# A compact triangular inverse on 32- and 64-row tiles, masks on VectorE, and part of the weights' low parts on GpSimd

## Chip, cores and metric

One NeuronCore of a Trainium2 chip runs the whole program as one launch. The metric is the device time in microseconds (us), the median of three runs. Engines by name: TensorE (PE, and PEld for its weight loads), VectorE (DVE), ScalarE (ACT), GpSimd (POOL), and SyncE (SP), which issues the transfers of the weights.

## What is computed

Two transformer blocks over 256 tokens of width 2048, in fp32. Block 1 mixes a gated linear recurrence, forgetting attention and a pooling branch, then a feed-forward of 5632. Block 2, which the change touches, mixes 16 heads of an RWKV-7 recurrence (head size 64) with 8 heads of a gated delta rule (GDN, head size 128), then projects out and runs a second feed-forward. Cut to what matters:

```python
h = rms_norm_2(x, attn_norm_w); proj = h @ w_in            # 2048 -> 3360 + 3088
y_a = rwkv7_mixer(proj[..., :N_RWKV_IN], ...)              # S = S*w + (S a) b^T + v k^T, y = S r
y_b = gdn_mixer(proj[..., N_RWKV_IN:N_IN], ...)            # chunked delta rule:
#   L = tril(k_beta k^T * gamma, -1); u, w = solve(I + L, [v_beta, k_beta * exp(g)])
x = x + concat([y_a, y_b]) @ w_out
x = x + (silu(h2 @ w_gate) * (h2 @ w_up)) @ w_down         # h2 = rms_norm_2(x, ffn_norm_w)
```

Both mixers are computed in chunks of 128 tokens. Each chunk of each head then needs the inverse of a 128x128 unit triangular matrix; the kernel calls the strictly triangular matrices `ab`, and four of them (two heads, two chunks) make one inverse step.

## The kernel before, in words

**Products.** Weights are streamed once, as tiles of 128 output columns by up to eight k-tiles of 128 (chunks of 128x1024 fp32). `weights` (L302) starts a chunk's transfer on SyncE, rounds it on ScalarE to a high part `hi` in fp32r (L314), and subtracts on VectorE to get the low part `lo` (L315, listed under L206). `product` multiplies: per k-tile, `step3` issues a 512-column matmul of hi against the activations' two parts and a 256-column matmul of lo against their high part. The rings hold 4 raw, 3 hi and 3 lo chunks. ScalarE and VectorE work on chunks ahead of TensorE by a priority offset (`ahead_mix`, 139 and 145 in the mixers).

**Order of the work.** In block 2 the program is written in sequence, and a list scheduler orders each engine's instructions at build time by priority and by its own estimate of times; `high_priority(offset=n)` moves what stands in it ahead of the code around it. At run time every engine works its list in order and waits on semaphores.

**The mixers** (`mixers`, L898) have four groups, each of two RWKV head pairs and then two GDN heads. For each: the projections (`rwkv_front`, `gdn_front`: the products, the token shift or convolution, the decay, the matrices `ab`), then `diagonals`, later `merged_inverse` and the back part (`rwkv_back`, `gdn_back`). The back part of one half group is issued beside the projections of the next, with `back_ahead` = 205; `diagonals` stands 129 ahead. There are 12 inverse steps: 8 for RWKV, 4 for GDN. The last GDN back part stands after `out2_first`, the first 12 k-tiles of the output projection (L1399); `out2_second` does the last 4.

**The inverse.** `diagonals` (L1098) sends the 16x16 diagonal blocks through DRAM, inverts them on VectorE, and brings them back as `cm`. `merged_inverse` (L1127) spreads these over a 128x128 block-diagonal `xt` with a mask on VectorE, transposes it to `x` on TensorE (L236) and copies that on ScalarE (L1139). Two levels follow, 16 and 32: VectorE masks `ab` to `off`, TensorE multiplies `off` by `x`, then the result `m1` by `xt` (four full 128x128 products each), and transposes the new `xt` (L1163; full tiles at level 16, 64x64 at level 32). For RWKV, VectorE adds the identity to `m1` and ScalarE copies `xt`; for GDN, ScalarE scales `m1` by beta and VectorE adds to `xt`. The last level joins the two 64-row halves with 64x64 products.

**GpSimd** does only small memsets in the mixers (L962, L1011, L1280), and adds squares in `out2_second`.

The lines that the core of the steps rests on:

```python
for lev in ("lev16", "lev32"):
    off = self.tp.tile([P, 4, P], F32, name="off", tag="w4")
    self.mul(off, full[:, p0:p0 + 4], self.bc(lev, 4))
    for q in range(4):
        self.mm(pm[:, q * P:(q + 1) * P], off[:, q], x[:, q])
```

Of the kernel before, what the change touches and what calls it, by code (L numbers as in the profile page):

```python
# [7 lines left out]
F32 = mybir.dt.float32  # L8
F32R = mybir.dt.float32r
AF = mybir.ActivationFunctionType  # L10
ALU = mybir.AluOpType
# [4 lines left out]
P = 128  # L16
S = 256
# [134 lines left out]
def constants():  # L152
    i = np.arange(P)
    r, c = i[:, None], i[None, :]
    sel1 = np.zeros((P, 8), np.float32)
    sel2 = np.zeros((P, 8), np.float32)
    for h in range(8):
        sel1[h, h] = 1.0
        sel2[32 + h, h] = 1.0
    c1 = ((i >= 32) & (i < 40)).astype(np.float32)[:, None]  # L160
    c2 = (i < 8).astype(np.float32)[:, None]
    up = (c > r).astype(np.float32)
    upi = (c >= r).astype(np.float32)
    same = lambda b: (r // b == c // b)
    lev = lambda b: (same(2 * b) & ~same(b) & (c > r)).astype(np.float32)
    return [
        ("ident", np.eye(P)), ("ones", np.ones((P, P))),
        ("causal", np.where(c <= r, 0.0, -1e30)), ("causalT", np.where(r <= c, 0.0, -1e30)),
        ("head64", same(64).astype(np.float32)),
        ("nsel1", -sel1), ("sel2", sel2), ("c1", c1), ("c2", c2),  # L170
        ("atmask", np.concatenate([up, upi], 1)),
        ("lev16", lev(16)), ("lev32", lev(32)), ("lev64", lev(64)), ("blk16", same(16).astype(np.float32)),
        ("id16", np.broadcast_to(np.eye(16).reshape(1, 256), (P, 256))),
    ]


def ffn_out(w):
# [5 lines left out]
class Prog:  # L183
# [83 lines left out]
    pieces = (4, 4, 4, 4)  # L267
    early = []
    parted = False
    narrow = nar3 = nar4 = False  # L270
    nar1 = nar2 = nar5 = True
    turn = 0
# [29 lines left out]
    def weights(self, src, nkt):  # L302

        parts = []
        ahead = self.ahead_mix if self.parted else (self.ahead[self.narrow],) * 2
        for k in range(0, nkt, 8):
            n = min(8, nkt - k) * P
            with self.tc.high_priority(offset=ahead[0]):
                raw = self.rawp.tile([P, n], F32, name="raw", tag="raw")
                self.nc.sync.dma_start(out=raw, in_=src[:, k * P:k * P + n])  # L310
            with self.tc.high_priority(offset=ahead[1]):
                hi = self.hip.tile([P, n], F32R, name="hi", tag="hi")
                lo = self.lop.tile([P, n], F32R, name="lo", tag="lo")
# [481 lines left out]
class Block2(Block1):  # L795
# [25 lines left out]
    def block2(self):  # L821
        rh = lambda k, h=self.h: h[:, k]
        with ExitStack() as st:
            self.yp = self.pool("y2", 1, st=st)
            self.y = self.moving(self.yp, 8, "y", at=self.AT["y"])
            self.yg = [None] * 8
            with ExitStack() as st2:
                self.mixers(rh, st2)
            xst = ExitStack()
            self.x = self.pool("xres", 1, st=xst, side="right").tile([P, KT, S], F32, name="xres", tag="xres")  # L830
            self.narrow = self.nar5
            self.out2_second()
        self.narrow = False
        with xst:
            self.ffn("wg2", "wd2", 1e-5, self.feed_out, "left")
            self.last_norm()
# [61 lines left out]
    def mixers(self, rh, st):  # L898
# [24 lines left out]
        for g in range(4):  # L923
            slots = self.rwkv_group(g, rh, w2)
# [8 lines left out]
            self.step(pend, first=True)  # L933
        self.narrow = self.nar4
        self.out2_first()
        self.step(pend)

    def step(self, pend, first=False):
# [14 lines left out]
                        self.gdn_back(g, fr, xx)  # L953

    back_ahead = 205
    diag_ahead = 129
    front_ahead = 0

    def shifted(self, ps, o, j):

        t = self.w(S + 1, "shf")
        self.G.memset(t[:, 0:1], 0.0)  # L962
# [42 lines left out]
    def rwkv_rest(self, j, slot, t, slots):  # L1005
        gp, sg = self.gp, self.sg[j]
        r, k, v = t

        ch = lambda z: z.rearrange("p (c t) -> p c t", c=2)
        cw, e1, e2 = (ch(self.w(2 * (P + 1), n)) for n in ("cw", "e1", "e2"))  # L1010
        self.G.memset(cw[:, :, 0:1], 0.0)  # L1011
# [86 lines left out]
    def diagonals(self, slots, gdn):  # L1098
# [25 lines left out]
        self.nc.sync.dma_start(out=cm, in_=scr2.rearrange("p b i j -> (b i) p j"))  # L1124
        slots["cm"] = cm

    def merged_inverse(self, slots, half, gdn):  # L1127

        full, cm, p0 = slots["ab"], slots["cm"], 4 * half
        q4 = lambda z: z.rearrange("p (q t) -> p q t", q=4)  # L1130
        xt = self.gp.tile([P, 4, P], F32, name="xt", tag="xt", bufs=2)
        x = self.gp.tile([P, 4, P], F32, name="xn", tag="xn", bufs=2)
        self.mul(xt.rearrange("p q (b j) -> p q b j", b=8),
                 cm[:, p0:p0 + 4].rearrange("p q (a j) -> p q a j", a=1).to_broadcast([P, 4, 8, 16]),
                 self.c("blk16").rearrange("p (a b j) -> p a b j", a=1, b=8).to_broadcast([P, 4, 8, 16]))
        px = self.psx_tile(True)
        for q in range(4):
            self.tr(px[:, q * P:(q + 1) * P], xt[:, q])
        self.A.copy(x, q4(px))  # L1139
        beta = lambda q, rows=slice(0, P): self.nbt[rows, q % 2, 2 * gdn + q // 2:2 * gdn + q // 2 + 1]  # L1140
        for lev in ("lev16", "lev32"):
            off = self.tp.tile([P, 4, P], F32, name="off", tag="w4")
            self.mul(off, full[:, p0:p0 + 4], self.bc(lev, 4))
            pm = self.psx_tile(True)
            for q in range(4):
                self.mm(pm[:, q * P:(q + 1) * P], off[:, q], x[:, q])
            m1 = self.tp.tile([P, 4, P], F32, name="m1", tag="w4")
            pt = self.psx_tile(True)
            if gdn is None:
                self.add(m1, q4(pm), self.bc("ident", 4))  # L1150
            else:
                for q in range(4):
                    self.act(m1[:, q], pm[:, q * P:(q + 1) * P], AF.Copy, scale=beta(q))
            for q in range(4):
                self.mm(pt[:, q * P:(q + 1) * P], m1[:, q], xt[:, q])
            if gdn is None:
                self.A.copy(xt, q4(pt))
            else:
                self.add(xt, q4(pt), xt)
            px = self.psx_tile(True)  # L1160
            n = P if lev == "lev16" else 64
            for q in range(4):
                self.T.transpose(px[:n, q * n:(q + 1) * n], xt[:n, q, :n], self.c("ident")[:n, :n])  # L1163
            self.A.copy(x[:n, :, :n], q4(px[:n, :4 * n]))

        lo, hi = slice(0, 64), slice(64, P)
        pm = self.psx_tile(True)
        for q in range(4):
            self.mm(pm[hi, q * 64:(q + 1) * 64], full[lo, p0 + q, hi], x[lo, q, lo])
        m1 = self.tp.tile([P, 4, P], F32, name="m1", tag="w4")  # L1170
        if gdn is None:
            self.A.copy(m1[hi, :, :64], q4(pm[hi, :S]))
        else:
            for q in range(4):
                self.act(m1[hi, q, :64], pm[hi, q * 64:(q + 1) * 64], AF.Copy, scale=beta(q, hi))
        for q in range(4):
            self.mm(pm[lo, S + q * 64:S + (q + 1) * 64], m1[hi, q, :64], xt[hi, q, hi])
        self.A.copy(xt[lo, :, hi], q4(pm[lo, S:]))
        return xt

# [89 lines left out]
    def gdn_front(self, i, rh, w2, slots):  # L1270
# [3 lines left out]
        for b in range(6):  # L1274
# [2 lines left out]
                self.scaled(ps, big[:, b])  # L1277
                continue
            t = self.w(S + 3, f"gc{b}")
            self.G.memset(t[:, :3], 0.0)  # L1280
            self.scaled(ps, t[:, 3:])
            ch = (i, 4 + i, 8 + 2 * i, 9 + 2 * i)[b]
            o = big[:, b]
# [152 lines left out]
```

## Time and profile before

| what | value |
|---|---|
| median of 3 runs | 2920.99 us (2920.43 to 2922.79) |
| the profiled execution | 2924.65 us, span 2922.9 us |
| TensorE busy | 2888.2 us (99%), 17676 matmuls |
| VectorE busy | 1990.9 us (68%) |
| ScalarE busy | 1506.3 us (52%) |
| GpSimd busy | 21.5 us (1%) |
| mean granted TensorE clock | 0.998 of full speed |

The span runs from the first to the last instruction of the profiled execution; its own time is 1.75 us longer. Durations in the trace are of that execution. A matmul's duration holds its way through the array, so neighbours overlap, and TensorE's pace is read from the starts of instructions in a row rather than from their durations.

### The profile page before, as it was taken

The numbers are of one execution on the slowest core, as the hardware profiler recorded it, in microseconds if no ns is written. First come the engines' busy times: TensorE is split into PE (matmuls) and PEld (weight loads), VectorE is DVE, ScalarE is ACT, GpSimd is POOL, SyncE is SP. The second block draws the span as 40 slices with busy tenths as digits, with TensorE's granted clock in tenths as the row PEclk, the third lists the DMA queues.
The fourth block names the chain that finished last, engine by engine and source line by source line (L and its number), as shares of the span: only waits on it lengthen the run. The fifth ranks groups of instructions, "written<-read, shape, count | busy, mean of one in ns | idle before, by whom it ended". The sixth has DMA issues, their size and how long they took to land. (4 is left out here: it accounts for less than half of the span.)

```text
span 2922.9 us, 46401 instructions
## 1 busy us (share of the span) xinstructions
PE 2888.2 (99%) x17676; PEld 2540.8 (87%) x17676; DVE 1990.9 (68%) x3393; ACT 1506.3 (52%) x2448; POOL 21.5 (1%) x88
## 2 busy tenths in 40 slices
PE   8999999999999999999999999999999999999998
PEld 8999988888888888888888878887888888888887
DVE  7855766666766665666667878888776665566665
ACT  6644454444554444444556555666564444444454
POOL 0000000000000000000000000000010000000000
PEclk9999999999999999999999999999999999999999
DMA  6544555555655556555565423233465555655554
GB/s 232 183 160 154 173 188 191 190 188 189 231 190 189 189 177 192 201 191 191 180 206 186 148 87 122 92 130 110 145 207 189 190 186 182 201 191 190 184 177 159
DMA packets 178047, 515.78 MB, mean 176 GB/s; under 512 B 32024, under 2 KB 59040, under 8 KB 177568
## 3 DMA queue, kind: packets, MB, share of 16 engines
q1 hardware_dynamic: 177536, 511.80, 51.9%
q8 instruction: 138, 2.26, 0.3%
q10 hardware_dynamic: 288, 1.02, 0.1%
q14 instruction: 85, 0.70, 0.1%
HBM read 505.66 MB, written 7.09 MB: 175 GB/s over the span
## 5 line engine op out<-in xcount | busy, mean ns | idle before, releaser
L233 PE MATMUL ps<-h,hi 128*128 128x512 f32 (+1 forms) x5904 | 1801.0, 366 | 1.2 <-DVE xp L206 0.9
L206 DVE TENSOR_TENSOR lo<-raw,hi 128x1024 fp32r<-128x1024 f32 (+2 forms) x1028 | 1156.6, 1125 | 759.0 <-ACT hi L314 754.9
L314 ACT CAST hi<-raw 128x1024 fp32r<-128x1024 f32 (+2 forms) x1028 | 997.2, 971 | 1193.3 <-issue 663.8
L233 PE MATMUL ps<-h,lo 128*128 128x256 f32 x5152 | 1410.6, 282 | 0.9 <-DVE lo L206 0.6
L233 PEld LDWEIGHTS ps<-h,hi 128*128 128x128 f32 x5904 | 1041.6, 188 | 164.4 <-issue 6.0
L233 PEld LDWEIGHTS ps<-h,lo 128*128 128x128 f32 x5152 | 969.5, 188 | 29.4 <-issue 2.4
L233 PE MATMUL ps<-mid,hi 128*128 128x512 f32 (+1 forms) x1452 | 486.2, 385 | 0.0
L233 PE MATMUL ps<-mid,lo 128*128 128x256 f32 x1408 | 386.1, 281 | 0.0
L233 PEld LDWEIGHTS ps<-mid,hi 128*128 128x128 f32 x1452 | 265.4, 188 | 50.5
L233 PEld LDWEIGHTS ps<-mid,lo 128*128 128x128 f32 x1408 | 265.1, 188 | 5.3
L206 DVE TENSOR_TENSOR t<-ps,s 128x256 f32<-128x256 f32 x323 | 134.8, 417 | 0.0
L381 ACT COPY s<-ps 128x256 f32<-128x256 f32 x323 | 118.3, 367 | 0.0
L233 PE MATMUL ps<-merged,hi 128*128 128x512 f32 x256 | 88.0, 392 | 0.0
L233 PE MATMUL ps<-merged,lo 128*128 128x256 f32 x256 | 69.0, 280 | 0.0
L233 PEld LDWEIGHTS ps<-merged,hi 128*128 128x128 f32 x256 | 47.0, 188 | 9.6 <-DVE merged L206 0.2
L233 PE MATMUL ps<-y,hi 128*128 128x512 f32 (+1 forms) x160 | 49.3, 359 | 1.7 <-ACT hi L314 1.4
L233 PEld LDWEIGHTS ps<-merged,lo 128*128 128x128 f32 x256 | 48.1, 188 | 1.3
L233 PE MATMUL ps<-yg,hi 128*128 128x512 f32 (+1 forms) x160 | 48.6, 354 | 0.0
L233 PE MATMUL ps<-yb,hi 128*128 128x512 f32 x128 | 46.1, 393 | 0.0
L233 PE MATMUL ps<-yc,hi 128*128 128x512 f32 x128 | 46.1, 393 | 0.0
L233 PE MATMUL ps<-ya,hi 128*128 128x512 f32 x128 | 45.9, 391 | 0.0
L206 DVE TENSOR_TENSOR t<-ps,xres 128x256 f32<-128x256 f32 x78 | 33.1, 424 | 12.9 <-PE ps L233 7.0
(383 smaller groups left out, 2307.8 us busy)
## 6 DMA issues: line engine op xcount, KB each, us to landing
raw<-wg SPq DMA_DIRECT2D x352, 512.0 KB, 4.2
raw<-w SPq DMA_DIRECT2D x292, 512.0 KB, 3.6
raw<-wd SPq DMA_DIRECT2D x128, 512.0 KB, 3.5
raw<-wbr SPq DMA_DIRECT2D x48, 512.0 KB, 3.5
raw<-wo SPq DMA_DIRECT2D x48, 512.0 KB, 4.3
raw<-wd SPq DMA_DIRECT2D x128, 192.0 KB, 3.1
raw<-wo SPq DMA_DIRECT2D x32, 256.0 KB, 3.2
xin<-x SPq DMA_DIRECT2D x4, 512.0 KB, 6.4
```

Source lines behind the costliest of these rows:

```text
L206: return (e or self.V).tensor_tensor(out=o, in0=x, in1=y, op=op)
L233: return self.T.matmul(o, lhsT=l, rhs=r, start=start, stop=stop, skip_group_check=True)
L314: self.A.copy(hi, raw)
L381: self.A.copy(s[:rows], ps[:rows, S:])
```

## The change

The two lower levels of the inverse work on compact tiles: level 16 on four 32x32 diagonal blocks of each matrix, level 32 on two 64x64 blocks. Both the inverse so far and its transpose are kept (`x[:, 0]` and `x[:, 1]`), so the transposes on TensorE go; the first one is VectorE's transpose of 32x32 blocks. The identity is added to `m` in both mixers, and a mask on VectorE spreads a level's blocks into the next tile. The masked `ab` (`off32`, `off64`) are made once per group in `diagonals`. While `shared` is set (from the start of the mixers to the end of `out2_second`), the last 256 columns of the low part of a chunk of over four k-tiles are subtracted on GpSimd. The small memsets go to VectorE, and the last back part gets priority 2000.

```diff
 constants():
-        ("lev16", lev(16)), ("lev32", lev(32)), ("lev64", lev(64)), ("blk16", same(16).astype(np.float32)),
+        ("id64", np.tile(np.eye(64), (2, 1))), ("id32", np.tile(np.eye(32), (4, 1))),
+        ("lev16", diag_blocks(lev(16), 32)), ("lev32", diag_blocks(lev(32), 64)),
+        ("blk16", diag_blocks(same(16).astype(np.float32), 32)), ("blk32", diag_blocks(same(32).astype(np.float32), 64)),
...
+def diag_blocks(m, n):
+    return np.concatenate([m[i:i + n, i:i + n] for i in range(0, P, n)], 0)
 setup():
-        self.cst = self.const.tile([P, a["cst"].shape[1]], F32, name="cst")
+        self.cst = self.const.tile([P, a["cst"].shape[1] + 224], F32, name="cst")[:, :a["cst"].shape[1]]
 weights():
-                self.sub(lo, raw, hi.bitcast(F32))
+                m = n - 2 * P if self.shared and n > 4 * P else n
+                self.sub(lo[:, :m], raw[:, :m], hi[:, :m].bitcast(F32))
+                if m < n:
+                    self.sub(lo[:, m:], raw[:, m:], hi[:, m:].bitcast(F32), self.G)
 mixers():
-        self.parted = True
+        self.parted = self.shared = True
...
         self.out2_first()
+        self.back_ahead = self.last_ahead
         self.step(pend)
...
+    last_ahead = 2000
 shifted(), rwkv_rest(), gdn_front():
-        self.G.memset(...)
+        self.V.memset(...)
 diagonals(), at its end:
+        for lev, w in (("lev16", 32), ("lev32", 64)):
+            off = slots[lev] = gp.tile([P, n, w], F32, name=f"off{w}", tag=f"off{w}_{n}")
+            for r in range(0, P, w):
+                r = slice(r, r + w)
+                self.mul(off[r], full[r, :, r], self.c(lev, r).rearrange("p (a t) -> p a t", a=1).to_broadcast([w, n, w]))
 merged_inverse(), in place of the spread, the transposes and the two levels:
+        def tiles(out, left, right, w, rows=P):
+            for q in range(4):
+                for r in range(0, rows, w):
+                    r = slice(r, r + w)
+                    self.mm(out[r, q], left[r, q], right[r, q])
+        def merge(x, lev, w, rows):
+            off = slots[lev][:, p0:p0 + 4]
+            pm = self.psx_tile(True)
+            tiles(q4(pm[:, :4 * w]), off, x[:, 1], w)
+            m = self.tp.tile([P, 4, 64], F32, name="m1", tag="m4", bufs=3)[:, :, :w]
+            if gdn is None:
+                self.add(m, q4(pm[:, :4 * w]), one(self.c(f"id{w}"), w))
+            else:
+                for q in range(4):
+                    self.stt(m[:, q], pm[:, q * w:(q + 1) * w], beta(q), self.c(f"id{w}"), ALU.mult, ALU.add)
+            pt = self.psx_tile(True)
+            pt = pt[:, :8 * w].rearrange("p (a q t) -> p a q t", a=2, q=4)
+            tiles(pt[:, 0], m, x[:, 0], w)
+            tiles(pt[:, 1], x[:, 0], m, w, rows)
+            return pt
+        xt = self.gp.tile([P, 4, P], F32, name="xt", tag="xt", bufs=2)
+        self.V.memset(xt[hi, :, lo], 0.0)
+        x = self.gp.tile([P, 2, 4, 32], F32, name="xa", tag="xa", bufs=2)
+        self.mul(x[:, 0].rearrange("p q (b j) -> p q b j", b=2),
+                 cm[:, p0:p0 + 4].rearrange("p q (a j) -> p q a j", a=1).to_broadcast([P, 4, 2, 16]),
+                 self.c("blk16").rearrange("p (a b j) -> p a b j", a=1, b=2).to_broadcast([P, 4, 2, 16]))
+        self.V.transpose(x[:, 1].rearrange("p q t -> p (q t)"), x[:, 0].rearrange("p q t -> p (q t)"))
+        pt = merge(x, "lev16", 32, P)
+        x = self.gp.tile([P, 2, 4, 64], F32, name="xb", tag="xb", bufs=1)
+        for j in range(2):
+            self.mul(x[:, j].rearrange("p q (b t) -> p q b t", b=2),
+                     pt[:, j].rearrange("p q (b t) -> p q b t", b=1).to_broadcast([P, 4, 2, 32]),
+                     self.c("blk32").rearrange("p (a b t) -> p a b t", a=1, b=2).to_broadcast([P, 4, 2, 32]))
+        pt = merge(x, "lev32", 64, 64)
+        for r in (lo, hi):
+            self.A.copy(xt[r, :, r], pt[r, 0])
+        y = self.tp.tile([P, 4, 64], F32, name="xc", tag="m4", bufs=3)
+        self.V.tensor_copy(y[lo], pt[lo, 1])
```

The join of the two halves that follows is as before, with `y` in place of `x` and a compact `m1`.

## Rows read from the trace of the kernel before

**Rows 1.** The page, part 1 (busy time of each engine).

```profile
PE 2888.2 (99%) x17676; PEld 2540.8 (87%) x17676; DVE 1990.9 (68%) x3393; ACT 1506.3 (52%) x2448; POOL 21.5 (1%) x88
...
PE 26%; DVE 0%; ACT 0%; DMA 0%; issue 0%; ACTq 0%; POOLq 0%; DVEq 0%
```

**Rows 2.** Stretches: us, then PE, PEld, DVE, ACT, POOL, clock, DMA.

```profile
1440.00:1460.00 20.00, 20.00 (x117) 17.63 (x116) 13.34 (x22) 11.09 (x18) 0.00 (x0) 1.00 0.67 212
...
1680.00:1700.00 20.00, 17.16 (x103) 14.45 (x102) 12.89 (x28) 10.97 (x25) 0.45 (x3) 0.91 0.32 105
...
1780.00:1800.00 20.00, 20.00 (x117) 17.60 (x116) 18.05 (x51) 11.34 (x14) 0.00 (x0) 1.00 0.56 191
...
2020.00:2040.00 20.00, 20.00 (x117) 17.58 (x117) 18.56 (x55) 10.76 (x14) 0.00 (x0) 1.00 0.48 156
...
1580.00:2144.00 564.00, 554.16 (x3446) 458.68 (x3445) 440.50 (x1086) 337.57 (x671) 5.25 (x48) 1.00 0.38 123
```

**Rows 3.** Waits of TensorE, 1575 to 2150 us, the longest group.

```profile
PE pb L236 <- DVE xt L206: 3.5, 4, 2.8
```

**Rows 4.** TensorE's weight loads, 1580 to 2144 us: count, busy us, mean ns, idle before.

```profile
L233 PEld LDWEIGHTS pb<-xt,m 128*128 128x128 f32 x192 | 25.1, 190 | 2.5 <-ACT m L230 1.1 <-issue 0.2
...
L236 PEld LDWEIGHTS pb<-cst,xt 128*128 128x128 f32 x48 | 5.9, 147 | 6.0 <-DVE xt L206 5.5
...
L233 PEld LDWEIGHTS pb<-xn,ab 64*64 64x64 f32 x64 | 4.3, 134 | 1.7 <-issue 1.0 <-ACT s L381 0.2 <-ACT xn L1164 0.2
...
L1163 PEld LDWEIGHTS pb<-cst,xt 64*64 64x64 f32 x48 | 3.0, 107 | 3.4 <-ACT xt L1157 1.7 <-DVE xt L206 1.1 <-issue 0.7
```

**Rows 5.** Timeline of one inverse: start us, us from first to last end, instructions.

```profile
1696.62 0.97 PEld L233 LDWEIGHTS pb<-xt,m 128*128 128x128 f32 x8
...
1699.90 0.39 PE L233 MATMUL ps<-h,hi 128*128 128x512 f32 x1
...
1700.22 0.54 PEld L233 LDWEIGHTS pb<-xn,ab 64*64 64x64 f32 x8 [0.24 <-ACT s L381]
...
1701.05 0.40 PE L233 MATMUL ps<-h,hi 128*128 128x512 f32 x1
```

**Rows 6.** Timeline of the RWKV front: column halves, then row halves.

```profile
1633.68 0.66 PE L233 MATMUL pf<-ak,tok 128*64 128x128 f32 x8
...
1629.11 0.69 PE L233 MATMUL pf<-ar,kt 64*128 64x256 f32 x4
...
1629.54 0.59 PE L233 MATMUL pf<-ar,bt 64*128 64x256 f32 x2
```

**Rows 7.** VectorE's operations by form, 1575 to 2150 us.

```profile
L206 DVE TENSOR_TENSOR lo<-raw,hi 128x1024 fp32r<-128x1024 f32 x111 | 135.3, 1220 | 32.7 <-ACT hi L314 32.5
...
L218 DVE SCALAR_TENSOR_TENSOR ak<-pf,cst 128x256 f32<-128x256 f32 x32 | 13.3, 416 | 0.0
...
L206 DVE TENSOR_TENSOR m<-pb,cst 128x512 f32<-128x512 f32 x16 | 10.9, 684 | 3.4 <-PE pb L233 3.2
...
L206 DVE TENSOR_TENSOR off<-ab,cst 128x512 f32<-128x512 f32 x16 | 10.9, 681 | 0.0
...
L206 DVE TENSOR_TENSOR ar<-r,e 128x128 f32<-128x128 f32 x16 | 4.5, 280 | 0.5 <-ACT e L230 0.5
...
L206 DVE TENSOR_TENSOR etmp<-d,e 32x63 f32<-32x63 f32 x8 | 1.7, 207 | 0.0
...
L206 DVE TENSOR_TENSOR sc<-e,e 128x1 f32<-128x1 f32 x8 | 1.2, 148 | 0.0
```

**Rows 8.** By form: GpSimd 1500 to 2200, VectorE 2144 to 2180, VectorE 700 to 860.

```profile
L206 POOL TENSOR_TENSOR acc<-acc,q 128x256 f32<-128x256 f32 x15 | 13.8, 920 | 154.7 <-ACT q L230 154.7
...
L218 DVE SCALAR_TENSOR_TENSOR h<-xres,par,h 128x256 fp32r<-128x256 f32 x16 | 11.3, 714 | 0.2
...
L218 DVE SCALAR_TENSOR_TENSOR h<-xres,par,h 128x256 fp32r<-128x256 f32 x16 | 7.7, 478 | 0.0
```

More of the change, by code (lines that the diff above doesn't have):

```diff
@@ L269 @@
     parted = False
+    shared = False
     narrow = nar3 = nar4 = False
@@ L832, in block2 @@
             self.out2_second()
-        self.narrow = False
+        self.narrow = self.shared = False
         with xst:
@@ L961, in shifted @@
         t = self.w(S + 1, "shf")
-        self.G.memset(t[:, 0:1], 0.0)
+        self.V.memset(t[:, 0:1], 0.0)
         self.scaled(ps, t[:, 1:])
@@ L1010, in rwkv_rest @@
         cw, e1, e2 = (ch(self.w(2 * (P + 1), n)) for n in ("cw", "e1", "e2"))
-        self.G.memset(cw[:, :, 0:1], 0.0)
+        self.V.memset(cw[:, :, 0:1], 0.0)
         for c in range(2):
@@ L1125, in diagonals @@
         slots["cm"] = cm
+        for lev, w in (("lev16", 32), ("lev32", 64)):
[3 more added lines that the diff above has]
+                self.mul(off[r], full[r, :, r], self.c(lev, r).rearrange("p (a t) -> p a t", a=1).to_broadcast([w, n, w]))
     def merged_inverse(self, slots, half, gdn):
         full, cm, p0 = slots["ab"], slots["cm"], 4 * half
+        lo, hi = slice(0, 64), slice(64, P)
@@ L1130, in merged_inverse @@
         q4 = lambda z: z.rearrange("p (q t) -> p q t", q=4)
[L1131 to L1136, printed above, removed]
@@ L1137, in merged_inverse @@
-        for q in range(4):
-            self.tr(px[:, q * P:(q + 1) * P], xt[:, q])
-        self.A.copy(x, q4(px))
-        beta = lambda q, rows=slice(0, P): self.nbt[rows, q % 2, 2 * gdn + q // 2:2 * gdn + q // 2 + 1]
-        for lev in ("lev16", "lev32"):
-            off = self.tp.tile([P, 4, P], F32, name="off", tag="w4")
-            self.mul(off, full[:, p0:p0 + 4], self.bc(lev, 4))
+        one = lambda z, w: z.rearrange("p (a t) -> p a t", a=1).to_broadcast([P, 4, w])
+        beta = lambda q, rows=slice(0, P): self.nbt[rows, q % 2, 2 * gdn + q // 2:2 * gdn + q // 2 + 1]
@@ L1144, in merged_inverse @@
+        def tiles(out, left, right, w, rows=P):
[5 more added lines that the diff above has]
+            off = slots[lev][:, p0:p0 + 4]
             pm = self.psx_tile(True)
-            for q in range(4):
-                self.mm(pm[:, q * P:(q + 1) * P], off[:, q], x[:, q])
-            m1 = self.tp.tile([P, 4, P], F32, name="m1", tag="w4")
@@ L1148, in merged_inverse @@
-            pt = self.psx_tile(True)
+            tiles(q4(pm[:, :4 * w]), off, x[:, 1], w)
+            m = self.tp.tile([P, 4, 64], F32, name="m1", tag="m4", bufs=3)[:, :, :w]
             if gdn is None:
-                self.add(m1, q4(pm), self.bc("ident", 4))
+                self.add(m, q4(pm[:, :4 * w]), one(self.c(f"id{w}"), w))
             else:
                 for q in range(4):
-                    self.act(m1[:, q], pm[:, q * P:(q + 1) * P], AF.Copy, scale=beta(q))
-            for q in range(4):
-                self.mm(pt[:, q * P:(q + 1) * P], m1[:, q], xt[:, q])
@@ L1156, in merged_inverse @@
[L1156 to L1166, printed above, removed]
+                    self.stt(m[:, q], pm[:, q * w:(q + 1) * w], beta(q), self.c(f"id{w}"), ALU.mult, ALU.add)
@@ L1167, in merged_inverse @@
+        pt = merge(x, "lev32", 64, 64)
[3 more added lines that the diff above has]
+        self.V.tensor_copy(y[lo], pt[lo, 1])
         pm = self.psx_tile(True)
         for q in range(4):
-            self.mm(pm[hi, q * 64:(q + 1) * 64], full[lo, p0 + q, hi], x[lo, q, lo])
-        m1 = self.tp.tile([P, 4, P], F32, name="m1", tag="w4")
+            self.mm(pm[hi, q * 64:(q + 1) * 64], full[lo, p0 + q, hi], y[lo, q])
@@ L1171, in merged_inverse @@
+        m1 = self.tp.tile([P, 4, 64], F32, name="m1", tag="m4", bufs=3)
         if gdn is None:
-            self.A.copy(m1[hi, :, :64], q4(pm[hi, :S]))
+            self.A.copy(m1[hi], q4(pm[hi, :S]))
         else:
             for q in range(4):
-                self.act(m1[hi, q, :64], pm[hi, q * 64:(q + 1) * 64], AF.Copy, scale=beta(q, hi))
+                self.act(m1[hi, q], pm[hi, q * 64:(q + 1) * 64], AF.Copy, scale=beta(q, hi))
         for q in range(4):
-            self.mm(pm[lo, S + q * 64:S + (q + 1) * 64], m1[hi, q, :64], xt[hi, q, hi])
+            self.mm(pm[lo, S + q * 64:S + (q + 1) * 64], m1[hi, q], xt[hi, q, hi])
@@ L1279, in gdn_front @@
             t = self.w(S + 3, f"gc{b}")
-            self.G.memset(t[:, :3], 0.0)
+            self.V.memset(t[:, :3], 0.0)
             self.scaled(ps, t[:, 3:])
```

## Prediction

> **What bounds the kernel now.** I read the page's busy shares and its chain first: TensorE is busy 99% of the span and the chain that ended last is TensorE's products [rows 1]. "Busy" here holds matmul latency, so I next read the table of stretches: a plain product stretch has 117 matmuls in 20 us, that is 0.34 us for a pair of one hi (512 columns) and one lo (256) [rows 2]. The mixers, the only place that the change touches, run from about 1580 to 2144 us: TensorE 554 of 564 us, VectorE 440, ScalarE 338, GpSimd 5 [rows 2]. Then the waits: TensorE's longest group there is 3.5 us, for the first block of the inverse [rows 3]; the stretch 1680 to 1700 that holds it also has the only lower granted clock, 0.91 (a mean of the two levels) against 1.00 elsewhere [rows 2]. So the mixers are bound by TensorE's instruction stream, with VectorE near 90% in places (18.05 and 18.56 of 20 us) [rows 2]. A microsecond taken off TensorE's stream is worth about one, while VectorE keeps up.
>
> **TensorE: what goes.** Each self.mm in fp32 is two instructions. An inverse (12 of them: 8 rwkv, 4 gdn) now issues 4 block transposes, and per level 4+4 products and 4 transposes; the last join (16 instructions of 64x64) stays. Price of one, from eight in a row: full tiles (0.97 - 0.19) / 7 = 0.111 us, 64x64 tiles (0.54 - 0.13) / 7 = 0.058 us [rows 4, 5]. A run of small tiles pays more than its instructions: from the hi before it to the second hi after it are 1.15 us (1699.90 to 1701.05), less the pair's 0.34 and 8 x 0.058 = 0.46, leaves 0.35 us per run for emptying and refilling the array [rows 2, 5]. Gone per inverse: 32 x 0.111 + 8 full transposes x 0.11 (taken at the full tiles' price) + one run of 4 small transposes (0.23 + 0.35) = 3.55 + 0.88 + 0.58 = 5.0 us; times 12 is 60 us (counts: 192, 192, 48, 48 and 48 [rows 4], the second 192 and the second 48 in rows of the same kind).
>
> **TensorE: what comes.** Level 16: 16 + 32 products on 32x32 tiles, 96 instructions; level 32: 8 + 8 + 4 on 64x64, 40 instructions; in four runs. 32 columns stand in no row. Serial price by the line through 0.111 and 0.058: about 0.031 us. Do tiles on different rows and columns of the array run side by side? Column halves do: eight 128x64 instructions take 0.66 us where eight full ones of the same length take 0.97 for their loads alone [rows 5, 6]. Row halves do: four in two tiles take 0.69 us, two in one tile 0.59 [rows 6]. The new tiles are diagonal, apart in both, and neighbours in issue order. Bounds: serial, 96 x 0.031 + 40 x 0.058 + 4 x 0.35 = 6.7 us per inverse, 80 us, a net +20; all tiles side by side (four of 32, two of 64; the last 8 instructions have one tile alone), 0.74 + 0.92 + 0.46 + 1.4 = 3.5 us, 42 us, a net -18; only pairs, 4.3 us, 51 us, a net -9. I take -18: it is what both rows of tiles show, carried from two to four.
>
> **VectorE.** Prices: 512 columns 0.68, 256 0.42, 128 0.28, 63 0.21, one column 0.15, a lo of 1024 1.22, so a lo of 768 between them 0.95 us [rows 7]. Masks move to the step of the diagonals: an rwkv group pays 4 x 0.42 + 2 x 0.68 for 4 x 0.68 before, +0.3; a gdn group 4 x 0.28 + 2 x 0.42 for 2 x 0.68, +0.6. Per inverse three operations of 512 go (-2.0). Come: block spread 0.28, the 32x32 transpose (in no row: 0.15 to 0.68, taken as 0.28 like any 128 columns), zeroing a quarter 0.28 to 0.42, merge one 0.28 (gdn: 4 x 0.21, ScalarE before), two spreads 0.84, merge two 0.42 (gdn 4 x 0.21), one copy 0.42: rwkv +0.8, gdn +1.8. Sum 4 x 0.9 + 8 x 0.8 + 4 x 1.8 = +17 us. 48 small memsets leave GpSimd for VectorE: +7; each needs a buffer that the multiply right behind it needs too, so little can be queued behind its wait. The low parts: 51 x 2 + 16 = 118 chunks of eight k-tiles lose 0.27 us each, -31. The chunks of four in out2_first and out2_second stay whole. TensorE's last two k-tiles of a chunk now wait for GpSimd, with all of its queue behind them: nothing, as 0.92 us [rows 8] beside 0.95 end together, bounds 0 and the hold below.
>
> **What sharing costs.** One GpSimd subtract of 128x256 takes about 0.92 us, 118 of them 109 us, on an idle queue [rows 8]. Where GpSimd now adds squares (2144 to 2180), VectorE's h operation, both tensors in SBUF, takes 714 ns against 478 in the first block without GpSimd: 16 x 0.236 = 3.8 us for 15 adds, some 0.25 each [rows 8]. VectorE gains 0.27 and loses 0.25 to 0.92 per chunk: net nothing to +77 us. I take 0.3, the measured case: 440 + 17 + 7 - 31 + 35 = 468 of about 546 us (564 less 18), 86%. The Trainium skill, "SBUF — State Buffer", section "Who interferes with whom", calls the ports that the two share an exclusive lock for a whole instruction; by that rule nearly every pair could meet whole, and the sum would be the first rival's. The trace agrees that there is a hold (714 against 478), but on average a quarter of one.
>
> What of it reaches TensorE? The two fullest kinds of stretch (18.05 and 18.56 of 20 us, four of them, at the diagonals of the rwkv groups) get 3 us of masks and some seven shared chunks: about 22 us of work in 20. The excess is covered by three buffers of low parts and by later slack; without that cover it is 2 us each. I charge 6 us, bounds 0 and 8.
>
> **No price.** ScalarE loses its copies of transposes and is far from full. PSUM tiles per inverse fall from 8 to 5. The last gdn step, moved ahead with last_ahead = 2000, issues no DMA; on TensorE, ScalarE and VectorE it passes out2_first's products, and cannot start before its blocks land. Nobody needs its output before out2_second at 2144, so nothing, bounds -2 and +2; if the products no longer fill its waits, it costs those 2. The first inverse still waits for the blocks' DMA (3.5 us, and about 1.8 of clock); were both gone, -5, which is the low end. The constants shrink, off any path.
>
> **Sum.** -18 + 6 = -12 us. The profiled execution is 2924.65 us (span 2922.9), 3.7 above the median of 2920.99; 2924.65 - 12 = 2912.7, on the median **2909**. Its own range: -23 (first wait gone too) to -4, 2898 to 2917.
>
> **Rivals.**
> - **Sharing makes VectorE the bound** in the rwkv stretches. Each subtract holds a VectorE operation whole: 118 x 0.92 = 109 us, 74 more than I took, and VectorE has 440 + 17 + 7 - 31 + 109 = 542 of 546 us. Low parts come late and TensorE, in order, waits; if a third of the 74 passes the buffers, 25 us come back: -18 + 25 = +7, 2928. By the same third it decides (18 us back) from a hold of (35 + 54) / 118 = 0.75 us a chunk. For it: 714 against 478, and VectorE waits for the same ScalarE cast as GpSimd, so they start together. Against: the lower measured mean. Chance 0.17.
> - **Diagonal tiles take turns.** All four write one PSUM bank; the row tiles of the trace write different banks by the code, the column tiles share a bank but no row border. Serial: +20 + 6 = +26, 2947. Chance 0.12. The Trainium skill, "TensorEngine Tiling (Array Packing)", section "Restrictions and Gotchas", says that different row tiles can't access one PSUM bank at once, which speaks for this rival; no run here shows it for diagonal tiles.
> - **Only pairs overlap**, as the rows literally show: -9 + 6 = -3, 2918. The change would then not do what it says at 32 rows. Chance 0.13.
>
> **Numbers.** The forecast has 0.58. A measurement of this kernel can tell about 0.2%, 5.8 us, from no change. Faster: the forecast but for 0.02, and a third of the pairs case: 0.60. Slower: the serial case and half of VectorE's: 0.20. Same: 0.20. For 8 in 10 the range takes the forecast, pairs and VectorE's case up to 2932; the serial case is left out.
>
> **What would show it.** Right: eight 32x32 instructions start within some 0.1 us; TensorE has about 18 us less in the mixers, with no new wait of over 1 us; lo rows show 128x768 on VectorE near 0.95 and 128x256 on GpSimd near 0.9; VectorE about 86%. Wrong: lo on VectorE well above 1.2 us mean, TensorE waiting on lo in a sum of over 15 us, 32x32 instructions evenly 30 ns apart, or several new stretches with a granted clock below 1.

## The result and the profile after

The change takes 2951.82 us (median of 4 runs, 2947.77 to 2954.20) against 2920.71 for the kernel before on the same chip: ratio 1.0104, interval 1.0092 to 1.0116. It is 31 us slower, where 12 us faster was forecast, and above the range. The profiled execution took 2950.39 us (span 2948.6).

First the page, part 1 and the first line of the chain, as in [rows 1]:

```profile
PE 2882.7 (98%) x18780; PEld 2526.1 (86%) x18780; DVE 2015.1 (68%) x3552; ACT 1481.2 (50%) x2388; POOL 158.6 (5%) x155
...
PE 87%; DVE 6%; issue 2%; DMA 2%; ACT 2%; POOL 0%; SPq 0%; ACTq 0%; POOLq 0%; DVEq 0%
```

TensorE has more instructions and less busy time than before, yet the span grew by 26 us. The chain passes over VectorE, "issue", DMA and ScalarE for 12% of the span, but it doesn't tell where the loss is: in run 1 below, which is faster than both kernels, it passes over them for 8%. (In [rows 1] it could be followed over the last 26% only, all of it TensorE's, so the two lines are not to be set against each other share by share.)

Next the mixers as one stretch, the view of [rows 2] (us, then PE, PEld, DVE, ACT, POOL, clock, DMA share, GB/s), from 1560 us to the first residual that out2_second adds. That moment is the same place in every kernel here, so the length of this stretch measures the mixers. The kernel before:

```profile
1560.00:2144.90 584.90, 575.06 (x3567) 476.86 (x3566) 458.04 (x1111) 350.20 (x690) 5.25 (x48) 1.00 0.38 126
```

and the changed one:

```profile
1560.00:2171.30 611.30, 570.46 (x4674) 462.33 (x4673) 480.85 (x1265) 324.76 (x627) 138.09 (x115) 0.97 0.39 120
```

The whole loss is here: 611.3 - 584.9 = 26.4 us. Length less PE busy is TensorE's idle time: 9.8 us before, 40.8 after. The clock went from 1.00 to 0.97, which over 611 us is some 37 us at the lower level. VectorE, the engine that was to be watched, is busy 480.85 of 611.3 us, 79%: it is not full. So TensorE loses by waiting and by its clock, and VectorE's sum doesn't explain it.

The waits of TensorE, 1560 to 2171 us, as [rows 3] (what waited, for what: sum, times, longest):

```profile
PE pf L240 <- DVE kp L225: 14.0, 7, 5.8
PE pb L240 <- DVE xa L1186: 10.4, 3, 5.4
PE ps L240 <- DVE lo L213: 4.1, 4, 2.9
PE pf L240 <- ACT sq L237: 2.8, 3, 1.3
```

The first is new and the second has grown. kp is an operand of the RWKV front, for which TensorE didn't wait before. xa is the first block tile of the inverse; its like before, xt, was waited for 3.5 us [rows 3]. Neither is a low part. TensorE hardly waits for low parts (4.1 us for VectorE's in the third line, and no line for GpSimd's); it waits for other work of VectorE.

One such place can be followed from end to end. GpSimd's timeline (start, us, ..., idle before and releaser):

```profile
1857.13 6.06 POOL L213 TENSOR_TENSOR lo<-raw,hi 128x256 fp32r<-128x256 f32 x1 [2.68 <-ACT hi L323]
```

SyncE's queue:

```profile
1844.88 10.87 SPq L319 DMA_DIRECT2D raw<-w  x3
1856.39 0.33 SPq L1136 DMA_DIRECT2D scs<-e  x1
1863.22 0.33 SPq L319 DMA_DIRECT2D raw<-w  x1
1863.64 0.39 SPq L1138 DMA_DIRECT2D cmp<-scs  x1
```

VectorE, at the start of that subtract and at the end of the gap:

```profile
1857.30 0.41 DVE L225 SCALAR_TENSOR_TENSOR kp<-kp,r 128x256 f32<-128x256 f32 x1
1857.63 0.41 DVE L213 TENSOR_TENSOR yy<-yy,rs_y 128x256 f32<-128x256 f32 x1
1857.97 0.94 DVE L213 TENSOR_TENSOR lo<-raw,hi 128x768 fp32r<-128x768 f32 x1
...
1867.93 0.29 DVE L213 TENSOR_TENSOR xa<-cmp,cst 128x128 f32<-128x128 f32 x1 [5.00 <-DMA cmp<-scs]
1868.14 0.48 DVE L225 SCALAR_TENSOR_TENSOR kp<-r,par,kp 128x256 f32<-128x256 f32 x1
```

TensorE:

```profile
1868.67 1.22 PE L240 MATMUL pf<-kp,cst 128*128 128x256 f32 x2 [5.79 <-DVE kp L225]
```

and the granted clock:

```profile
1863.00:1868.00 5.00, 0.00 (x0) 0.00 (x0) 0.07 (x1) 0.00 (x0) 1.56 (x3) 0.94 0.74 207
1868.00:1885.00 17.00, 16.26 (x173) 10.71 (x173) 6.85 (x22) 1.69 (x4) 0.00 (x0) 0.52 0.13 42
```

Read them in order. A subtract that takes 0.72 us at its fastest stands on GpSimd for 6.06, while VectorE runs operation on operation, mostly with both inputs in SBUF. Its raw buffer is free only at 1863.2, and the next load raw<-w waits for it at the head of SyncE's queue. Behind that load stands the diagonals' read cmp<-scs (1863.64). VectorE sits 5.00 us in front of xa, which needs cmp; kp, which does not, is behind it; TensorE waits 5.79 us for kp, and then runs near half clock for 17 us (0.52, so almost all of it at 1.2 GHz). One late subtract ends in a stop of TensorE of 5.8 us and a slow stretch behind it.

It does so with the help of the order that the scheduler gave to this kernel. In VectorE's list of run 1 below, the same kp stands 19 operations ahead of xa, and xa finds its blocks there:

```profile
1839.45 0.47 DVE L225 SCALAR_TENSOR_TENSOR kp<-r,par,kp 128x256 f32<-128x256 f32 x1
...
1846.40 0.28 DVE L213 TENSOR_TENSOR xa<-cmp,cst 128x128 f32<-128x128 f32 x1
```

So this one place shows how a late subtract reaches TensorE, but not that the lateness alone would have.

### The profile page after: what moved, and what is told of

Its sections match the earlier page's. It is cut to its first block, busy times and chain, and to the rows that moved or that the text cites. A ratio compares the mean times of both kernels' runs of the same rounds, so it can differ in the third digit from the quotient of the medians.

```text
span 2948.6 us, 48876 instructions
## 1 busy us (share of the span) xinstructions
PE 2882.7 (98%) x18780; PEld 2526.1 (86%) x18780; DVE 2015.1 (68%) x3552; ACT 1481.2 (50%) x2388; POOL 158.6 (5%) x155
## 4 chain that ended last, share of the span: by engine, by line
PE 87%; DVE 6%; issue 2%; DMA 2%; ACT 2%; POOL 0%; SPq 0%; ACTq 0%; POOLq 0%; DVEq 0%
PE ps L240 80%; PE pb L240 4%; PE pf L240 3%; DVE lo L213 2%; ACT hi L323 1%; DVE gbig L225 1%; DMA scs<-e 1%; DVE e L213 1%; DVE etmp L213 1%; PE pf L243 0%; DMA xo<-xs 0%; POOL lo L213 0%; DMA cmp<-scs 0%; DMA par<-par 0%; DMA raw<-wo 0%
## 5 line engine op out<-in xcount | busy, mean ns | idle before, releaser
L213 DVE TENSOR_TENSOR lo<-raw,hi 128x1024 fp32r<-128x1024 f32 (+3 forms) x1028 | 1129.1, 1098 | 751.7 <-ACT hi L323 747.9
L213 POOL TENSOR_TENSOR lo<-raw,hi 128x256 fp32r<-128x256 f32 x118 | 142.5, 1210 | 1709.9 <-ACT hi L323 1616.0
```

Of the source, the lines that this page charges most:

```text
L213: return (e or self.V).tensor_tensor(out=o, in0=x, in1=y, op=op)
```

## The experiments

Ratios are to the kernel before on the same chip, with 95% intervals. "Mixers" is the length of the stretch above in the profiled execution of each run.

**1. The change without the sharing.** In mixers():

```diff
-        self.parted = self.shared = True
+        self.parted = True
```

> The changed kernel with every low part whole on VectorE; the compact inverse, the memsets on VectorE and the priority of the last part stay. Theory A (GpSimd's subtract holds VectorE's operations that read two SBUF tensors, the chains of the diagonals and of the RWKV front get late, TensorE waits and its clock drops): TensorE's 18 us gain shows, 2903 to 2913 us, and the small operations of the diagonals fall back from 0.41 to 0.21 us. Theory B (the compact inverse's own masks, spreads and memsets load VectorE): still above 2940 us. Theory C (both need each other): 2920 to 2935.

Measured: 2907.89 us, 0.9939 [0.9923, 0.9956]. The mixers as a stretch, then TensorE's longest waits:

```profile
1560.00:2127.40 567.40, 556.77 (x4661) 452.74 (x4660) 464.21 (x1262) 325.43 (x628) 0.00 (x0) 1.00 0.43 128
```

```profile
PE pb L240 <- DVE xa L1186: 4.5, 4, 1.9
PE ps L240 <- ACT s L393: 1.4, 1, 1.4
```

Without the sharing the change gains 16.6 us and beats both kernels. The mixers are 17.5 us shorter than before, all of it TensorE's busy time (575.06 to 556.77) with its idle time unchanged (10.6 against 9.8). The sharing costs the rest: 611.3 - 567.4 = 43.9 us, of which 30.2 are idle time and 13.7 longer busy time at the lower clock. VectorE is fuller here (464.21 of 567.4, 82%) than with sharing (79%), and TensorE waits no more than before. The small operations of the diagonals take 0.19 us on the mean of 240, and 0.25 with sharing, not the 0.41 that the expectation started from.

The small tiles do run side by side. TensorE's timeline of the first inverse (start, us from first to last end):

```profile
1683.27 0.45 PE L240 MATMUL pb<-xa,off 32*32 32x32 f32 x32
...
1685.07 0.45 PE L240 MATMUL pb<-xa,m 32*32 32x32 f32 x32
```

32 instructions start and end within 0.45 us, their starts 7 ns apart at the median; one after the other at the estimated 0.031 us they would need 0.99.

**2. The sharing alone, in the kernel before.** weights() of before gets the change's split, everything else stays:

```diff
-                self.sub(lo, raw, hi.bitcast(F32))
+                m = n - 2 * P if self.shared and n > 4 * P else n
+                self.sub(lo[:, :m], raw[:, :m], hi[:, :m].bitcast(F32))
+                if m < n:
+                    self.sub(lo[:, m:], raw[:, m:], hi[:, m:].bitcast(F32), self.G)
```

> The kernel before with one edit: the last 256 columns of the low parts of 1024 go to GpSimd in the mixers. Theory A: slower than before by the loss of the changed kernel plus TensorE's gain, 31 + 18 = 49 us, so 2950 to 2970 us, with several stretches at the lower clock. Theory B: VectorE is relieved, 2915 to 2922. Theory C: a small loss, 2922 to 2935.

Measured: 2958.94 us, 1.0114 [1.0099, 1.0129]. TensorE's longest wait is again the first block of the inverse, now 15.1 us in place of the 3.5 of [rows 3]:

```profile
PE pb L236 <- DVE xt L206: 15.1, 5, 4.9
```

The sharing costs 34 us with the old inverse too: it needs nothing of the compact one to hurt, and here kp stands ahead of xt in VectorE's list wherever the two are near each other.

**3. The memsets back on GpSimd**, sharing kept (three lines of this kind):

```diff
-        self.V.memset(t[:, 0:1], 0.0)
+        self.G.memset(t[:, 0:1], 0.0)
```

> The changed kernel with the 48 small memsets back on GpSimd, so that they stand in one queue with the subtracts. Theory A: VectorE gets 7 us back but GpSimd's queue now sits in front of the fronts' first writes; 2945 to 2960. If the memsets on VectorE were a cause of the loss: under 2940.

Measured: 2942.93 us, 1.0061 [1.0046, 1.0076], just below what was expected: moving the memsets to VectorE costs some 12.6 us (1.0104 - 1.0061 of 2921) by the timed runs and 6.9 by the mixers of the profiled executions (611.3 - 604.4) while the low parts are shared. Run 8 tells whether that holds without sharing.

**4. The last part's distance back to 205**, sharing kept:

```diff
-    last_ahead = 2000
+    last_ahead = 205
```

> The changed kernel with the last back part at 205 as before, instead of 2000. Theory A: nothing, 2949 to 2955. If the moved last part costs: a gain of over 3 us, all of it after 2060 us.

Measured: 2980.84 us, 1.0188 [1.0173, 1.0204]: 25 us worse than the change. A term that I had put at nothing is one of the largest; run 7 takes it apart.

**5 and 6. GpSimd beside VectorE, with nobody waiting for what it makes.** Both start from run 1 (VectorE makes every low part). A GpSimd subtract into columns that nobody reads stands where the shared one stood; run 5 reads the high part alone, run 6 also the raw weights and so holds their buffer:

```diff
                 self.sub(lo[:, :m], raw[:, :m], hi[:, :m].bitcast(F32))
+                if self.parted and n > 4 * P:
+                    self.sub(self.dummy, hi[:, n - 224:].bitcast(F32), hi[:, n - 224:].bitcast(F32), self.G)
```

and in run 6 `raw[:, n - 224:]` as the first input. As `parted` stays set, these extra subtracts also run in the stage behind the mixers; from the first residual to the end the spans are 778.6 and 780.7 us against 778.2 in run 1, so the mixers' stretch is the cleaner measure.

> The change without the sharing (VectorE makes every low part), and beside it GpSimd subtracts 224 columns of each mixer chunk's high part from themselves into a tile that nobody reads: GpSimd works as often and nearly as long as in the change, but holds no raw buffer and nothing waits for it. Against 0.994 of the kernel before for the change without sharing and 1.010 with it. Theory A (two engines reading and writing at once slow each other, and the slow VectorE is what TensorE waits for): most of the loss is here, ratio 1.003 to 1.012, and the small operations of VectorE at 0.35 us as in the change. Theory B (the loss is the raw buffer that GpSimd gives back late, and with it SyncE's queue): ratio 0.994 to 0.998. Theory C (TensorE waits for GpSimd's part of the low halves): ratio 0.992 to 0.996.

> The same, but GpSimd subtracts 224 columns of the high part from the raw weights, again into a tile that nobody reads: it now holds each raw buffer until it is done, and TensorE still waits for nothing of it. Theory A: as the run that reads the high part alone, within 0.003. Theory B: ratio 1.005 to 1.012, and SyncE waits at the weights' load for GpSimd. Theory C: ratio 0.992 to 0.997 again.

Measured: run 5 2925.55 us, 1.0006 [0.9996, 1.0015]; run 6 2937.40 us, 1.0047 [1.0032, 1.0063]. The mixers of run 5, with SyncE's longest waits at the weights' load:

```profile
1560.00:2143.40 583.40, 561.26 (x4652) 454.70 (x4651) 490.72 (x1262) 325.18 (x626) 136.53 (x115) 0.99 0.43 124
```

```profile
SPq L321 <- DVE lo L213: 198.6, 63, 9.4
```

and of run 6:

```profile
1560.00:2157.40 597.40, 569.94 (x4655) 459.45 (x4654) 502.03 (x1262) 325.22 (x627) 139.54 (x115) 0.98 0.42 122
```

```profile
SPq L321 <- DVE lo L213: 351.3, 114, 10.7
SPq L321 <- POOL cst L213: 26.0, 48, 1.1
```

None of the three theories holds alone. Run 5 falls below the interval that A gave for the two engines' contention and above B's; run 6 just misses B's, and lies 0.0041 above run 5 where A allowed 0.003. The stretch goes 567.4 (no GpSimd), 583.4 (contention), 597.4 (GpSimd reads the raw weights and holds their buffer), 611.3 us (the change): three steps of 16.0, 14.0 and 13.9 us; TensorE's idle time (length less PE busy) goes 10.6, 22.1, 27.5, 40.8.

The first two steps arise while the kernel runs and not from another order: from 1400 us to the first residual VectorE, ScalarE and SyncE do the same operations in runs 5 and 6 as in run 1 and in the same order, but for one pair of neighbours on VectorE in run 6. The first is contention; run 5's subtract also holds the high part, for which ScalarE waited 20 us, but TensorE waits 0.3 us for high parts there.

The second step is not shown to be the raw buffer. The lines above name who ended SyncE's waits, not how long it stood: over all lines it stands 389.3 us at the weights' loads in run 5, 400.0 in run 6 and 377.8 in run 1, and the waits that GpSimd ended are 26.0 us, at most 1.1 at a time. Reading two tensors also makes GpSimd's subtract longer, 662 ns at its shortest in place of 558, and VectorE is held longer beside it: its operations other than low parts and memsets take 377.4 us in run 1, 399.7 in run 5, 408.2 in run 6 and 416.4 in the change, in step with the stretch. So the 14.0 us may be the held buffer or more of the same contention, and no run tells these apart.

The third step mixes more. TensorE's low parts now come in part from GpSimd, VectorE is relieved of a quarter of each chunk, and the scheduler makes another list: of VectorE's 1438 operations in that stretch at most 1010 stand in the order of run 1. What each does to the 13.9 us wasn't measured.

**7. The last part's distance without the sharing**: run 1 with last_ahead = 205.

> The change without the sharing, and with the last part moved ahead by 205 in place of 2000. With sharing this setting cost 25 us. Theory D (the alternation of small tiles with the products' matmuls costs that, by the changes of tile shape and the clock that falls meanwhile, whoever makes the low parts): 2925 to 2940 us, ratio 1.000 to 1.005, and a stretch at half clock of some 30 us between 2100 and 2170 us. Theory E (it cost that only because the low parts came late): 2904 to 2914 us, ratio 0.992 to 0.997.

Measured: 2939.44 us (2933.70 to 2947.58), 1.0060 [1.0036, 1.0083]: theory D, and a little beyond it. The profiled execution, at 2935.78, is one of the faster ones. The mixers, then the stretch around the last inverse:

```profile
1560.00:2155.40 595.40, 585.85 (x4656) 466.02 (x4655) 464.47 (x1262) 325.44 (x628) 0.00 (x0) 0.97 0.42 121
...
2100.00:2110.00 10.00, 10.00 (x37) 5.37 (x36) 1.14 (x2) 0.00 (x0) 0.00 (x0) 0.50 0.26 79
2110.00:2120.00 10.00, 10.00 (x35) 5.67 (x36) 1.54 (x4) 1.47 (x2) 0.00 (x0) 0.50 0.10 26
```

TensorE is busy all the time and does 37 matmuls in 10 us, where run 1 does 59 in the same stretch. This is a loss of another kind: no idle time (9.5 us), 29 us more busy. Its timeline shows why:

```profile
2083.99 0.24 PE L240 MATMUL pb<-xa,off 32*32 32x32 f32 x2
2084.16 0.51 PE L240 MATMUL ps<-y,hi 128*128 128x512 f32 x1
2084.60 0.24 PE L240 MATMUL pb<-xa,off 32*32 32x32 f32 x2
2084.77 0.38 PE L240 MATMUL ps<-y,lo 128*128 128x256 f32 x1
2085.09 0.24 PE L240 MATMUL pb<-xa,off 32*32 32x32 f32 x2
2085.26 0.75 PE L240 MATMUL ps<-y,hi 128*128 128x512 f32 x1
...
2086.94 0.80 PE L240 MATMUL ps<-y,hi 128*128 128x512 f32 x1
...
2088.66 0.80 PE L240 MATMUL ps<-y,hi 128*128 128x512 f32 x1
```

The scheduler deals the small tiles out two at a time between the products' matmuls. From one hi to the next are 1.10 us (2084.16 to 2085.26) where a pair of hi and lo takes 0.34 [rows 2]: 0.76 for two runs of two small tiles, 0.38 each, the 0.35 that the prediction had found for a run. The matmuls' records hold 134 runs of small tiles in the mixers here and 89 in run 1. The 45 more are an estimated 17 us at 0.38. The clock falls to half at 2085.3 and stays there for 37.5 us; the same pattern then takes 1.72 us from hi to hi (2086.94 to 2088.66), so by an estimate this stretch would have taken 37.5 x 1.10 / 1.72 = 24 us at the full clock, and 13.5 us are the clock's. The two make 30.5, for 29 measured. (I had expected the half clock between 2100 and 2170 us, for some 30.) At a distance of 2000 the last inverse keeps its tiles in runs of up to 32.

**8. The memsets on GpSimd, without the sharing.**

> The change without the sharing, and with the memsets of the rows' first columns back on GpSimd. With sharing that gave some 12 us back. Theory F (the memsets stand on VectorE in front of operations that TensorE waits for): 2897 to 2903 us, ratio 0.990 to 0.993. Theory G (they only cost where VectorE is slowed by GpSimd, and beside an unslowed VectorE they are hidden): 2904 to 2912 us, ratio 0.993 to 0.996.

Measured: 2908.06 us, 0.9946 [0.9931, 0.9961], as run 1: theory G. Beside an unslowed VectorE the 48 memsets cost nothing; what run 3 gave back is part of the sharing's price. Run 8 also shows that another order need not cost: at most 1091 of VectorE's 1390 operations stand as in run 1. And with the memsets on GpSimd the sharing costs the same with either inverse: 1.0061 - 0.9946 = 0.0115 here, 0.0114 in run 2.

**9. The distance alone, in the kernel before**: `self.back_ahead = 2000` behind out2_first().

> The kernel before, with nothing of the change but the last part's distance: 2000 in place of 205. Theory H (that distance matters only where 32-row and 64-row tiles would alternate with the products; the matrices before are 128 rows high): ratio 0.998 to 1.002. Theory I (moving the last part ahead gains by itself, so that some of the 0.994 of the change without sharing is not the compaction's): ratio 0.993 to 0.997.

Measured: 2925.77 us, 1.0001 [0.9991, 1.0010]. Theory H: the distance is worth nothing by itself, so run 1's gain is the compaction's, on the condition that its last part is kept together.

**10. Half the share**: 128 columns of each chunk on GpSimd.

```diff
-                m = n - 2 * P if self.shared and n > 4 * P else n
+                m = n - P if self.shared and n > 4 * P else n
```

> The change with 128 of 1024 columns of each mixer chunk on GpSimd in place of 256, so that each of its subtracts is about half as long. None was 0.994 of the kernel before, all 256 was 1.010. If the loss goes by how long both engines work at once: half of it, ratio 1.000 to 1.004. If it goes by the number of GpSimd's instructions that can be held up or that a ring waits for: nearly all of it, ratio 1.005 to 1.011. If only the long ones hurt: ratio 0.994 to 0.999.

Measured: 2922.22 us, 0.9992 [0.9983, 1.0002]. A third of the loss (0.0053 of 0.0165) for half of the columns, between "half" and "only the long ones".

**11. Every part moved ahead by 2000**, without the sharing (`back_ahead = 2000`).

> The change without the sharing, and with every inverse's part moved ahead by 2000, not the last one alone. If small tiles still alternate with the products around the other inverses and pay for it: 2890 to 2903 us, ratio 0.987 to 0.992. If those are whole already at 205, because the work beside them is that of the mixers and not a long product: 2904 to 2912 us, ratio 0.993 to 0.996. If the part now stands in front of work whose operands are there, and TensorE waits in order: over 2912 us, ratio above 0.996.

Measured: 2913.69 us, 0.9965 [0.9953, 0.9976], slower than run 1. The runs of small tiles hardly fall (86 for 89), so those inverses were whole already, and TensorE now idles 16.9 us in the mixers for 10.6. The third case is the nearest.

**12. One tensor read on GpSimd in place of two**: run 5 with a copy.

```diff
-                    self.sub(self.dummy, hi[:, n - 224:].bitcast(F32), hi[:, n - 224:].bitcast(F32), self.G)
+                    self.G.tensor_copy(self.dummy, hi[:, n - 224:].bitcast(F32))
```

> As the run in which GpSimd reads the high part and nobody reads what it makes (ratio 1.0006, GpSimd's subtract 1176 ns at the mean), but GpSimd copies those 224 columns instead: one tensor read in place of two, as many instructions, nothing else changed. Theory J (what slows VectorE is any GpSimd instruction that reads and writes beside it, by its duration): GpSimd's copy takes 0.7 to 1.2 us, the small operations of VectorE at the diagonals stay near 0.25 us or above, ratio 0.998 to 1.002. Theory K (it is the two tensors that GpSimd reads): the small operations at 0.2 us as without sharing, ratio 0.993 to 0.996.

Measured: 2914.00 us (2910.96 to 2924.16), 0.9975 [0.9964, 0.9986], between the theories: half of run 5's loss by the timed runs, 3 of 16 us by the mixers of the profiled execution, which was one of the fastest. The small operations of the diagonals take 0.20 us on the mean, 0.22 in run 5. The copy is not only one tensor less, it is shorter, 373 ns at its fastest in place of 558, so this run doesn't decide between the two either.

## Why the prediction was wrong

**TensorE's terms held.** Forecast -18; run 1 has -18.3 us of PE busy time and -17.5 of length. Diagonal tiles run side by side, so the serial rival and the one where only pairs overlap fall. The small tiles come in 89 runs rather than the 72 that follow from six per inverse (four new, two of the last join). At the prediction's 0.35 us the 17 more would cost 6 us, and what gave them back wasn't taken apart, so part of this agreement is luck. Two slips in the text decided nothing: the hi at 1701.05 is the next one behind the run of small tiles, not the second, which is why only one pair is taken off; and the terms' bounds as they stand give -18 + 8 + 2 = -8 for the slow end of the range, not -4.

**VectorE's sum held.** Masks and spreads were put at +17 and memsets at +7; summed instruction by instruction, run 1 has +14.5 and +2.9 (a memset takes 60 ns, not the 150 of one column); neighbours overlap by a little, so its busy time grows by 6.2 only. The low part of 768 columns takes 983 ns on the mean for an assumed 950. From run 1 to the change VectorE gains 115 x 0.27 = 31 us and still ends 16.6 us higher (480.85 - 464.21): held for an estimated 48 us, 0.41 per chunk for the 0.3 that I took, inside my bounds. Of these, 39 show directly, in the operations other than low parts and memsets (416.4 - 377.4).

**The step that failed** is "What of it reaches TensorE?": 6 us, "covered by three buffers of low parts and by later slack", bounds 0 and 8. In the mixers the sharing measured 43.9 us; 30 of them come with the lists of run 1 (the steps of runs 5 and 6). I asked whether VectorE's work fits into the stretch, and it does, with a fifth to spare. What counts is when single operations end. A held operation stands at the head of an in-order queue, and the low parts' buffers cover low parts, not kp and xa behind them. I also gave GpSimd a price for itself (0.92 us) and none for its lateness: I had not followed the raw buffer's release, and through it SyncE's queue with the diagonals' reads, which the trace shows at one place. That GpSimd's part would cost nothing, "as 0.92 us [rows 8] beside 0.95 end together", rests on the same price; GpSimd's part took 1014 ns in the middle and 6063 at worst:

```profile
L213 POOL TENSOR_TENSOR lo<-raw,hi x115: 717/1014/6063, 1560.9 to 2160.5; 128x256 fp32r<-128x256 f32 x115
```

Of the prediction's four signs of being wrong only the last came, the stretches with a lower clock. VectorE's low parts took 983 ns on the mean, TensorE didn't wait on them for over 15 us, and the small tiles start 7 ns apart: I had watched the low parts, and the loss went past them.

**The first rival** had the right sign and place, but not the mechanism: it made VectorE's sum the bound, at 542 of 546 us, and its price of +7 us is far below the +26 of the trace.

**The moved last part, put at nothing** (bounds -2 and +2), holds for the change as it is, and for the wrong reason. I looked at what it passes in the queues, not at what it is dealt between: with compact tiles, leaving it at 205 costs 25 us with the sharing and 35 without (0.9939 to 1.0060). The 0.35 us per run of small tiles that would have told it stood in my own text.

**Left open.** Why the clock stays low for 17 us after one stall and for 3.4 after others wasn't settled, nor whether the second step is the raw buffer's or VectorE's, nor how the last 13.9 us divide between late low parts, the longer lateness of GpSimd and the other order of the lists. That the diagonals' reads are held by SyncE's order is read from the trace at one place; giving them another queue was not tried.

## What to carry to other kernels

Before work is moved to an idle engine, list the buffers that it will hold and the in-order queues that wait for those buffers, and follow them to the bound engine; a busy share below 80% on the helping engines protected nothing here. Look at the order of the lists too, which such a change makes anew. Small tiles on diagonal blocks of TensorE's array cost little while they stand in long runs (32 in 0.45 us) and, in run 7, about 0.38 us for every time that they are broken up by a large one, so compaction and its place in the order are one change. The version to keep is the compact inverse with its last part moved ahead and every low part on VectorE: 2907.89 us, 0.6% under the kernel before.

## What the runs showed of the hardware

VectorE is held by GpSimd where all its inputs lie in SBUF, and not where one lies in PSUM. Three groups of VectorE in the changed kernel (count, then min/median/max in ns):

```profile
L213 DVE TENSOR_TENSOR rs_w<-rs_w,rs_q x32: 405/418/968, 1618.5 to 2151.9; 128x256 f32<-128x256 f32 x32
L213 DVE TENSOR_TENSOR sc<-e,e x8: 140/151/692, 1614.9 to 2018.5; 128x1 f32<-128x1 f32 x8
L213 DVE TENSOR_TENSOR t<-ps,s x51: 359/408/425, 1567.2 to 2064.0; 128x256 f32<-128x256 f32 x51
```

rs_w and sc, both inputs in SBUF, lose up to 550 and 541 ns, whatever their size (256 columns or one). t, with one input in PSUM, is never held: 425 ns at most in 51. The same holds for all 308 operations of this stretch with an input in PSUM: none is over 10 ns longer than the longest of its kind in run 1. An operation with a single input in SBUF is not always free: one of the eight copies mid<-cw takes 693 ns, where run 1 has 170 at most.

How long a hold lasts shows where a small operation starts just behind a subtract:

```profile
1853.71 0.74 POOL L213 TENSOR_TENSOR lo<-raw,hi 128x256 fp32r<-128x256 f32 x1 [2.47 <-DVE e L213]
1853.73 0.77 DVE L213 TENSOR_TENSOR etmp<-d,e 32x28 f32<-32x28 f32 x1
```

This etmp takes 0.17 us at the median; here it ends with the subtract. The Trainium skill, "SBUF — State Buffer", section "Who interferes with whom", says that a VectorE instruction with at most one SBUF input, outside the two-port modes, doesn't contend, that one with two contends with a GpSimd instruction that reads SBUF, and, of the two-port modes, that whoever issues first has the shared ports for its whole instruction. The trace agrees on t and on rs_w (the profile doesn't tell the mode of the copy mid<-cw), and shows the hold to the end of the instruction for etmp too, which has two inputs in SBUF. A shorter instruction holds for a shorter time: VectorE's longest hold, against run 1, is 593 ns in the change, 500 in run 6, 404 in run 5, 299 in run 10 and 197 in run 12, where GpSimd's shortest instruction takes 717, 662, 558, 448 and 373.

The hold goes the other way too, and worse: a queue of VectorE operations without gaps kept one GpSimd subtract for 6.06 us, eight times its shortest 0.717. There the first to start did not have its way: fourteen VectorE operations that started behind the subtract (kp at 1857.30 to kt at 1862.19) ran at their usual length while it stood. Half the columns on GpSimd (run 10) still take 725 ns in the middle and up to 2753:

```profile
L213 POOL TENSOR_TENSOR lo<-raw,hi x115: 448/725/2753, 1559.6 to 2133.6; 128x128 fp32r<-128x128 f32 x115
```

The granted clock fell while TensorE was busy without a gap in its records, in run 7, where small tiles and products alternate: 1.00 before 2085, 0.50 from 2100 to 2120 us with PE busy 10.00 of 10.
